# A hybrid RWKV-7 and pooling layer: the diagonal blocks of a chunk inverse picked and placed by DMA, and a decay polynomial in squared factors

## Chip, cores and metric

The kernel runs on one core of one Trainium2 chip. The metric is device time in microseconds (us) of one launch. Times of instructions are from one profiled execution; times of the kernel are medians of several runs.

## The reference, cut to what matters

One decoder layer over 1024 tokens of width 1024, in float32. The part that the change touches is the RWKV-7 time mixing of 8 heads of 64 channels:

```python
w_log = -jax.nn.softplus(-(w0 + jnp.tanh(wd) @ wl_up)) - 0.5
decay = jnp.exp(-jnp.exp(w_log))
...
def step(S, inp):
    r_t, w_t, k_t, v_t, a_t, b_t = inp
    Sa = jnp.einsum('bhvk,bhk->bhv', S, a_t)
    S = S * w_t[:, :, None, :] + Sa[..., None] * b_t[:, :, None, :] + v_t[..., None] * k_t[:, :, None, :]
    y = jnp.einsum('bhvk,bhk->bhv', S, r_t)
    return S, y
...
m = jnp.mean(y, axis=-1, keepdims=True)
var = jnp.mean(jnp.square(y - m), axis=-1, keepdims=True)
y = (y - m) * lax.rsqrt(var + GN_EPS) * lnx_g + lnx_b
```

Around it stand an input layer norm and projection, a pooling group, the output projection with its layer norm, a SwiGLU FFN with a gated embedding, and a last layer norm.

## The kernel before, in words

The program is written with tiles and pools; a scheduler orders the instructions of each engine ahead of time, and each engine, and the SP queue that issues nearly all DMAs, then works in that fixed order. `solve` is given high priority by the scheduler.

The recurrence runs in chunks of 64 tokens (`NC` = 8 chunks to a half sequence of 512). Work comes as eight tasks t = 0 to 7: four pairs of heads (`p`, 128 channels) for each half sequence (`s`). `fr(t)` projects or reloads r, k, v and calls `front`; `solve` is called for two tasks at a time, so there are four solves, called pair 0 to 3 here, and inside one the loop variable `q` (0 or 1) counts the two tasks. While a solve waits, the PE (TensorE) has projection matmuls `pz` to run and, towards the end of the phase, the output projection's `pm`.

- `front` (L352 to L423): the decay is a polynomial of degree six of a tanh `t1`. ACT makes the first factor (L369), five scalar_tensor_tensor steps on DVE follow (L371), ACT adds the constant (L375) and two scans on DVE make the running products (L377, L381).
- `gram` (L425 to L450): small matmuls `pg`, each evicted through a mask by DVE into `gB` and `gK` (L439).
- `inverse` (L452 to L532): in `gB` lies, for each of 16 chunk-and-head blocks of one task, a strictly triangular 64x64 matrix. Its four 16x16 diagonal blocks are inverted directly, 128 of them side by side, one to a partition. To get there DVE masks the matrix (`dg`, L462), folds it to 16 columns (`dc`, L464), a DMA writes `dc` to a DRAM scratch (L466), a second DMA reads it back regrouped into `ab` (L467), and DVE takes the diagonal blocks out of `gB` (L468). After the small steps on `ab` and `ef` (L478 to L502), one DMA for each task writes both the inverse and its transpose (L506), another reads them as `cc` (L508), and DVE spreads `cc` into the block-diagonal tiles `fx` and `ex` with a mask (L511). Then come 64x64 matmuls `pn` and `pzz` (L524 to L532).
- `chain` (L534 to L585): for each chunk in turn the matmuls `cw`, `cu`, `cs`, with a DVE copy or update between them.
- `post` (L587 to L606): group norm. ACT takes a reciprocal root of the variance (L596), DVE refines it by a Newton step (L597 to L599), scales `py` (L600), and applies gain, bias and gate (L601, L604).

Of the kernel before, what the change touches and what calls it, by code (L numbers as in the profile page):

```python
# [23 lines left out]
NC = 8  # L24
# [3 lines left out]
LN_EPS = 1e-5  # L28
GN_EPS = 1e-5 * 64

DECAY = [7.38403150e-01, -2.23932079e-01, 3.39554149e-02, -3.43247040e-03,
         2.60245296e-04, -1.58445669e-05, 7.95516283e-07]

MU, W0, A0, KK, KA, RK, LG, LB, PS, IG, IB, MG, MB = 0, 14, 18, 22, 26, 30, 34, 38, 42, 46, 54, 62, 70
NCOL = 78
# [7 lines left out]
def hybrid_layer(ctx, tc, x, pT, w_in, cols, rows, lora, gl, pool_w, w_out,  # L43
# [32 lines left out]
    for h in range(2):  # L76
        r = slice(64 * h, 64 * h + 64)
        G.affine_select(out=gmask[r, 0:64], in_=gmask[r, 0:64], pattern=[[1, 64]],
                        compare_op=ALU.is_gt, fill=0.0, base=0, channel_multiplier=-1)
        G.affine_select(out=gmask[r, 64:128], in_=gmask[r, 64:128], pattern=[[1, 64]],  # L80
                        compare_op=ALU.is_ge, fill=0.0, base=0, channel_multiplier=-1)
        G.affine_select(out=bmask[r, :], in_=bmask[r, :], pattern=[[-16, 4]],
                        compare_op=ALU.is_ge, fill=0.0, base=0, channel_multiplier=1)
        G.affine_select(out=bmask[r, :], in_=bmask[r, :], pattern=[[16, 4]],
                        compare_op=ALU.is_ge, fill=0.0, base=15, channel_multiplier=-1)
    e0 = cq.tile([128, 65 * NC + 1], F32, name="e0")
    V.memset(e0, 0.0)
    V.memset(e0[:, 0:65 * NC + 1:65], 1.0)
# [4 lines left out]
    V.memset(epsl, LN_EPS)  # L93
    epsg = cq.tile([128, 1], F32, name="epsg")
    V.memset(epsg, GN_EPS)
    qb = cq.tile([128, 2], F32, name="qb")
    V.memset(qb[:, 0:1], DECAY[5])
    V.memset(qb[:, 1:2], DECAY[0])

    col = cp.tile([128, NCOL], F32, name="col")  # L100
    nc.scalar.dma_start(col, cols)
# [8 lines left out]
    V.tensor_scalar(hka, col[:, KA:KA + 4], 0.5, None, ALU.mult)  # L110
    oka = cq.tile([128, 4], F32, name="oka")
    V.tensor_scalar(oka, col[:, KA:KA + 4], -0.5, 1.0, ALU.mult, ALU.add)
    lor = cq.tile([128, 512], F32, name="lor")
    glw = cq.tile([128, 512], F32, name="glw")

# [58 lines left out]
    with pa:  # L174
# [20 lines left out]
        def kb(name):  # L195
            return s1.tile([128, NC, 64], F32, name=name, tag="kb", bufs=3)
# [155 lines left out]
        def front(pair, q, p, s, r, k, v):  # L352
# [22 lines left out]
            S.activation(wx3[:, :, 1:65], v3(pc), AF.Identity, bias=qb[:, 1:2])  # L375
# [49 lines left out]
        def gram(pr):  # L425
# [14 lines left out]
            for q, d in enumerate(pr["t"]):  # L440

                bk = d["bk"]
                for g in range(2):
# [5 lines left out]
                                mm(pk[R, o:o + 64], bk[R, 4 * g + i, 64 * x:64 * x + 64], ident[R, 64 * h:64 * h + 64], True, True)  # L449
                    S.copy(kt2[:, q, 4 * g:4 * g + 4, :].rearrange("p c t -> p (c t)"), pk)  # L450

        def inverse(pr):  # L452

            gB = pr["gB"]
            abf = s1.tile([128, 272], F32, name="ab", tag="ab", bufs=1)
            ab = abf[:, 0:256].rearrange("b (s t) -> b s t", t=16)
            QR = HR
            for q in range(2):
                A4 = gB[:, q, :, 0:64].rearrange("p c (q t) -> p c q t", q=4)
                dg = kb("dg")  # L460
                dg4 = dg.rearrange("p c (q t) -> p c q t", q=4)
                V.tensor_tensor(dg4, A4, bmask[:, None, :, None].to_broadcast([128, NC, 4, 16]), ALU.mult)  # L462
                dc = s1.tile([128, NC, 16], F32, name="dc", tag="dc", bufs=2)
                V.tensor_reduce(dc, dg.rearrange("p c (q t) -> p c t q", q=4), AX.X, ALU.add)  # L464
                d1 = dp.tile([NC, 128, 16], F32, name="d1", tag="d1", bufs=4)
# [12 lines left out]
            for t in range(1, 4):  # L478
                tv = tm[:, 0:4 * t * t].rearrange("b (q i s) -> b q i s", q=4, s=t)
                V.tensor_tensor(tv, e4[:, :, 0:t, 0:t],  # L480
                                a4[:, :, None, 0:t, t].to_broadcast([128, 4, t, t]), ALU.mult)
                V.tensor_reduce(e4[:, :, 0:t, t:t + 1], tv, AX.X, ALU.add)

            def off(lo, n):

                mi, hi = lo + n, lo + 2 * n
                tv = tm[:, 0:n * n * n].rearrange("b (i t s) -> b i t s", t=n, s=n)
                w = e[:, mi:hi, lo:mi]
                V.tensor_tensor(tv, e[:, lo:mi, None, lo:mi].to_broadcast([128, n, n, n]),
                                ab[:, lo:mi, mi:hi].rearrange("b s t -> b t s")[:, None]  # L490
                                .to_broadcast([128, n, n, n]), ALU.mult)
# [12 lines left out]
            for q in range(2):  # L504
                d2 = dp.tile([2 * NC, 128, 16], F32, name="d2", tag="d2", bufs=4)
                nc.sync.dma_start(d2.rearrange("(x c) (a i) t -> (c a) x (i t)", x=2, i=16), ef[QR[q]])  # L506
                cc = s1.tile([128, 2 * NC, 16], F32, name="cc", tag="cc", bufs=2)
                nc.sync.dma_start(cc, d2.rearrange("g p t -> p g t"))  # L508
                E_, F_ = [s1.tile([128, NC, 64], F32, name=n, tag=n, bufs=2) for n in ("ex", "fx")]
                for i, t in ((1, F_), (0, E_)):  # L510
                    V.tensor_tensor(t.rearrange("p g (q t) -> p g q t", q=4),  # L511
                                    cc[:, NC * i:NC * i + NC, None, :].to_broadcast([128, NC, 4, 16]),
                                    bmask[:, None, :, None].to_broadcast([128, NC, 4, 16]), ALU.mult)
                EF.append((E_, F_))

            def diag(l, rr, nm):
                ps = psb(nm)
                for c in range(NC):
                    for R in HR:
                        mm(ps[R, 64 * c:64 * c + 64], l[R, c, :], rr[R, c, :], True, True)  # L520
                return v3(ps)


            for q, (E_, F_) in enumerate(EF):  # L524
                S.copy(F_, diag(gB[:, q, :, 0:64], F_, "pn"))
            rr = [E_ for E_, _ in EF]
            for i in range(3):
                for q, (E_, n1) in enumerate(EF):
                    pz = diag(n1, rr[q], "pzz")
                    if i != 1:  # L530
                        rr[q] = kb("rr") if i == 0 else gB[:, q, :, 0:64]
                    V.tensor_tensor(rr[q], pz, E_, ALU.add)  # L532
# [54 lines left out]
        def post(d, py):  # L587
# [13 lines left out]
            V.scalar_tensor_tensor(ys, ys, col[:, LG + p:LG + p + 1], d["bv"], ALU.mult, ALU.add)  # L601
# [572 lines left out]
```

## Time and profile before

| | before |
|---|---|
| median of 3 runs | 1360.7 us (1359.55 to 1363.9) |
| the profiled execution | 1362.55 us |
| its span | 1360.8 us |
| busy: PE, DVE, ACT, POOL | 96%, 75%, 39%, 1% |
| mean granted TensorE clock | 0.985 |
| DMA | 177.72 MB, 119405 packets, 34944 of them under 512 B |

Busy time of PE is modelled from matmuls that overlap, so a PE that is busy all the time need not be at its peak rate. The projections, the time mixing and the pooling end with the last `pm` at 594 us; the FFN follows, and its matmuls run back to back. The solves lie between 123 and 564 us.

### The profile page before, as it was taken

Reading aid. Unit: us, or ns where it says so; the run is one execution under the profiler, and the core shown is the slowest. Engines: PE = TensorE matmul, PEld = TensorE weight load, DVE = VectorE, ACT = ScalarE, POOL = GpSimd, SP = SyncE. Lnnn points to the kernel's source line nnn. Section 1 sums busy time; section 2 is a strip of 40 time slices with the busy share of each in tenths; the row PEclk is TensorE's granted clock in tenths of the full one; section 3 lists DMA queues with packets and bytes.
Section 4 is the critical chain, followed back from the end, with each engine's and each line's share of the span. In section 5 each row is a group of like instructions: output and inputs, shape, how many; then the busy total and the mean of one; then the engine's idle time right before and its main releaser. Section 6 shows DMA issues by size and latency. Waiting matters only on the chain.

```text
span 1360.8 us, 22957 instructions
## 1 busy us (share of the span) xinstructions
PE 1310.2 (96%) x9028; PEld 1033.7 (76%) x9028; DVE 1025.9 (75%) x1807; ACT 528.6 (39%) x889; POOL 12.7 (1%) x48
## 2 busy tenths in 40 slices
PE   7999999998997999989999999999999999999997
PEld 5787777776765667767888888888888888887886
DVE  6947566579698873557799999777667777988768
ACT  6723432244334521156634332333333334553530
POOL 0000000000000000000000000000000000000000
PEclk9999989999998999989999999999999999999999
DMA  8621130122124251475423346322232336997813
GB/s 275 221 102 51 54 75 10 59 78 61 35 57 119 83 150 55 133 235 185 148 94 123 101 139 210 131 101 102 79 107 101 102 123 218 322 310 251 268 33 124
DMA packets 119405, 177.72 MB, mean 131 GB/s; under 512 B 34944, under 2 KB 44160, under 8 KB 119296
## 3 DMA queue, kind: packets, MB, share of 16 engines
q1 hardware_dynamic: 119152, 176.20, 39.6%
q8 instruction: 71, 1.16, 0.3%
q14 instruction: 38, 0.31, 0.1%
q10 hardware_dynamic: 144, 0.04, 0.0%
HBM read 126.13 MB, written 50.07 MB: 129 GB/s over the span
## 4 chain that ended last, share of the span: by engine, by line
PE 72%; DVE 13%; DMA 10%; ACT 2%; issue 2%; SPq 0%; DVEq 0%; ACTq 0%
PE p L49 31%; PE pz L49 10%; PE py L49 6%; PE pgt L49 6%; PE px L49 4%; PE pm L49 3%; DMA wdr<-ff_down 2%; PE pg L49 2%; DMA o<-h_d 1%; PE cw L49 1%; PE pzz L49 1%; DMA ar<-a_d 1%; PE pe L49 1%; PE cs L49 1%; DMA m_d<-o 1%
## 5 line engine op out<-in xcount | busy, mean ns | idle before, releaser
L49 PE MATMUL p<-tb,p 128*128 128x512 f32 x1056 | 250.1, 392 | 0.0
L49 PEld LDWEIGHTS p<-tb,p 128*128 128x128 f32 x1056 | 198.5, 188 | 44.4
L49 PE MATMUL p<-h,p 128*128 128x512 f32 x792 | 191.1, 394 | 0.0
L49 PE MATMUL pz<-hT,wh 128*128 128x512 f32 x576 | 189.1, 403 | 0.0
L49 PEld LDWEIGHTS p<-h,p 128*128 128x128 f32 x792 | 149.2, 188 | 34.8
L792 ACT CAST p<-a 128x512 fp32r<-128x512 f32 x132 | 81.3, 622 | 183.6 <-PE p L49 145.4
L49 PEld LDWEIGHTS pz<-hT,wh 128*128 128x128 f32 x576 | 107.1, 188 | 31.8 <-issue 4.7
L49 PE MATMUL pz<-hT,wl 128*128 128x512 f32 x288 | 116.6, 405 | 0.0
L793 DVE TENSOR_TENSOR p<-a,p 128x512 fp32r<-128x512 f32 x132 | 89.3, 686 | 15.3 <-ACT p L792 14.9
L49 PE MATMUL pm<-wo,mh 128*128 128x512 f32 x224 | 77.3, 413 | 2.4 <-DVE o L751 1.4
L949 DVE TENSOR_TENSOR u<-p,u 128x512 f32<-128x512 f32 x66 | 45.3, 686 | 31.3 <-PE p L49 31.2
L49 PEld LDWEIGHTS pz<-hT,wl 128*128 128x128 f32 x288 | 54.0, 188 | 15.4 <-issue 3.8
L49 PE MATMUL px<-da 128*128 128x512 f32 x276 | 64.2, 389 | 0.0
L49 PEld LDWEIGHTS px<-da 128*128 128x128 f32 x276 | 51.8, 188 | 10.8
L49 PE MATMUL pgt<-wg,h 128*128 128x512 f32 x192 | 51.1, 412 | 2.7 <-ACT wg L792 2.6
L49 PEld LDWEIGHTS pm<-wo,mh 128*128 128x128 f32 x224 | 41.4, 188 | 14.6 <-DVE o L751 1.8
L235 DVE TENSOR_TENSOR wl<-wr,wh 128x512 fp32r<-128x512 f32 x36 | 24.7, 688 | 32.9 <-ACT wh L233 32.1
L49 PE MATMUL py<-da 128*128 128x512 f32 x204 | 47.6, 389 | 0.0
L49 PEld LDWEIGHTS pgt<-wg,h 128*128 128x128 f32 x192 | 37.4, 197 | 12.1 <-ACT wg L792 3.0
L49 PE MATMUL pm<-wo,ml 128*128 128x512 f32 x112 | 46.0, 413 | 0.0
L49 PEld LDWEIGHTS py<-da 128*128 128x128 f32 x204 | 38.3, 188 | 8.0
L970 DVE TENSOR_TENSOR gs<-p,u 128x512 f32<-128x512 f32 x44 | 30.3, 690 | 18.2 <-PE p L49 17.6
(321 smaller groups left out, 2342.4 us busy)
## 6 DMA issues: line engine op xcount, KB each, us to landing
ar<-a_d SPq DMA_DIRECT2D x77, 256.0 KB, 4.0
wdr<-ff_down SPq DMA_DIRECT2D x55, 256.0 KB, 3.9
a<-ff_gate SPq DMA_DIRECT2D x44, 256.0 KB, 2.8
a<-ff_up SPq DMA_DIRECT2D x44, 256.0 KB, 2.8
a_d<-s SPq DMA_DIRECT2D x44, 256.0 KB, 2.3
b<-ff_down SPq DMA_DIRECT2D x22, 512.0 KB, 5.5
wr<-w_in SPq DMA_DIRECT2D x36, 256.0 KB, 2.9
a_d<-gs SPq DMA_DIRECT2D x33, 256.0 KB, 2.2
```

The costliest lines, as they stand in the source:

```text
L49: PE.matmul(o, lhsT=l, rhs=r, start=a, stop=z)
L235: V.tensor_tensor(wl, wr, wh.bitcast(F32), ALU.subtract)
L792: S.copy(h, r)
L793: V.tensor_tensor(l, r, h.bitcast(F32), ALU.subtract)
L949: V.tensor_tensor(t, ps, u, ALU.add)
L970: V.tensor_tensor(d, ps, u, ALU.add)
```

## The change

Three edits, in `inverse`, `front` and `post`.

- In `inverse` the four DVE steps that pick and place the diagonal blocks go. Two DMAs for each task (one for each half of the partitions) write the 64x64 matrices from `gB` to a DRAM scratch with a row length of 64 words and 64 words of padding to a matrix, so that a view with a pitch of 1040 words meets just the diagonal blocks; one DMA reads them from there into `ab`. On the way back four DMAs for a pair write the blocks into four DRAM images `d2`, whose other words were set to zero once, ahead of the loop, and eight DMAs read whole 64-column rows into `ex` and `fx`. Off-diagonal cleaning of `gB` is one multiply by a mask `omask` for each task; it has to wait until the DMAs that read `gB` have ended.
- In `front` the decay polynomial is a product of squared terms: four ACT steps and two DVE steps in place of one and five.
- In `post` the Newton step takes the square from ACT: two DVE steps in place of three.

```diff
+        d2 = [[dp.tile([2 * NC * HS], F32, name=f"d2{q}{x}", bufs=1) for x in range(2)] for q in range(2)]
+        zt = s1.tile([128, 2 * NC * HS // 128], F32, name="zt", tag="k2", bufs=KA_BUFS)
+        G.memset(zt, 0.0)
+        for q in range(2):
+            for x in range(2):
+                nc.scalar.dma_start(d2[q][x].rearrange("(p r) -> p r", p=128), zt)
...
+        def rows_of(d, h):
+            return d.rearrange("(c h r) -> c h r", c=NC, h=2)[:, h, 0:64 * 64].rearrange("c (p t) -> p c t", t=64)
+        def blocks_of(d):
+            return d.rearrange("(g r) -> g r", g=64)[:, 0:1024].rearrange("g (s t) -> g s t", t=64)[:, :, 0:16]
...
-                V.tensor_tensor(dg4, A4, bmask[:, None, :, None].to_broadcast([128, NC, 4, 16]), ALU.mult)
-                V.tensor_reduce(dc, dg.rearrange("p c (q t) -> p c t q", q=4), AX.X, ALU.add)
-                nc.sync.dma_start(d1.rearrange("c p t -> p c t"), dc)
-                nc.sync.dma_start(abf[QR[q], 0:256], d1.rearrange("c (a s) t -> (c a) (s t)", a=8))
-                V.tensor_tensor(gB[:, q, :, 0:64], gB[:, q, :, 0:64], dg, ALU.subtract)
+                for h, R in enumerate(HR):
+                    nc.sync.dma_start(rows_of(d1, h), gB[R, q, :, 0:64])
+                nc.sync.dma_start(abf[QR[q], 0:256].rearrange("g (s t) -> g s t", t=16), blocks_of(d1))
...
-                nc.sync.dma_start(d2.rearrange("(x c) (a i) t -> (c a) x (i t)", x=2, i=16), ef[QR[q]])
-                nc.sync.dma_start(cc, d2.rearrange("g p t -> p g t"))
-                for i, t in ((1, F_), (0, E_)):
-                    V.tensor_tensor(t.rearrange("p g (q t) -> p g q t", q=4),
-                                    cc[:, NC * i:NC * i + NC, None, :].to_broadcast([128, NC, 4, 16]),
-                                    bmask[:, None, :, None].to_broadcast([128, NC, 4, 16]), ALU.mult)
+            for i in (1, 0):
+                for q in range(2):
+                    nc.sync.dma_start(blocks_of(d2[q][i]), ef[QR[q], i, :].rearrange("g (i t) -> g i t", t=16))
+                for q in range(2):
+                    for h, R in enumerate(HR):
+                        nc.sync.dma_start(EF[q][i][R], rows_of(d2[q][i], h))
+            for q in range(2):
+                V.tensor_tensor(gB[:, q, :, 0:64], gB[:, q, :, 0:64],
+                                omask[:, None, :].to_broadcast([128, NC, 64]), ALU.mult)
...
-            S.activation(pc, t1, AF.Identity, scale=DECAY[6], bias=qb[:, 0:1])
-            for n in (0.0, DECAY[4], DECAY[3], DECAY[2], DECAY[1]):
-                V.scalar_tensor_tensor(pc, pc, n, t1, ALU.add, ALU.mult)
+            S.activation(pc, t1, AF.Square, bias=qb[:, 0:1])
+            S.activation(pd, t1, AF.Square, bias=qb[:, 1:2])
+            S.activation(pd, pd, AF.Identity, bias=qb[:, 3:4])
+            S.activation(t1, t1, AF.Square, bias=qb[:, 2:3])
+            V.scalar_tensor_tensor(pc, pc, QE[0], pd, ALU.add, ALU.mult)
+            V.scalar_tensor_tensor(pc, t1, QE[2], pc, ALU.add, ALU.mult)
...
-            V.scalar_tensor_tensor(ys, pvv, GN_EPS, y0, ALU.add, ALU.mult)
-            V.scalar_tensor_tensor(ys, ys, -0.5, y0, ALU.mult, ALU.mult)
-            V.scalar_tensor_tensor(y0, ys, 1.5, y0, ALU.add, ALU.mult)
+            S.activation(ys, y0, AF.Square)
+            V.scalar_tensor_tensor(ys, pvv, GN_EPS, ys, ALU.add, ALU.mult)
+            V.scalar_tensor_tensor(y0, ys, 3.0, y0, ALU.subtract, ALU.mult)
```

Since the scheduler orders everything anew, rows also move. On the SP queue of pair 0, where the inverse goes out and comes back (`d_...` and `d2` are the DRAM scratch, `wr` a weight load for `pz`), there stood before:

```order
L616 DMA rkv_d<-k_1421 128x512
L506 DMA d_2130<-ef 64x2x256
L506 DMA d_2138<-ef 64x2x256
L231 DMA wr<-w_in 128x512
L508 DMA cc<-d_2130 128x16x16
L508 DMA cc<-d_2138 128x16x16
L616 DMA rkv_d<-v_1493 128x512
```

and now there stands (744 and 745 are the inverse and the transpose of the first task, 746 and 747 those of the second):

```order
L639 DMA rkv_d<-k_1439 128x512
L531 DMA d_744<-ef 64x16x16
L531 DMA d_745<-ef 64x16x16
L531 DMA d_747<-ef 64x16x16
L531 DMA d_746<-ef 64x16x16
L534 DMA ex<-d_744 64x8x64
L534 DMA fx<-d_745 64x8x64 x2
L534 DMA fx<-d_747 64x8x64 x2
L534 DMA ex<-d_744 64x8x64
L534 DMA ex<-d_746 64x8x64 x2
L639 DMA rkv_d<-v_1511 128x512
```

Twelve issues stand together where there were four, and the weight load that stood among them has moved behind. The other three pairs have the same twelve in a row.

On DVE, at the end of the gram of pair 0's second task (`gB`, `gK` are evictions of gram blocks, `tm` is the first small step on `ab`), there stood before:

```order
L439 TENSOR_TENSOR gB<-pg_1985,gmask 128x512
L439 TENSOR_TENSOR gK<-pg_1995,gmask 128x512
L462 TENSOR_TENSOR dg<-gB,bmask 128x512
L439 TENSOR_TENSOR gK<-pg_2005,gmask 128x512
L464 TENSOR_REDUCE dc<-dg 128x128
L468 TENSOR_TENSOR gB<-gB,dg 128x8x64
L480 TENSOR_TENSOR tm<-ef,ab 128x4
```

and now:

```order
L450 TENSOR_TENSOR gB<-pg_2005,gmask 128x512
L242 TENSOR_TENSOR wl<-wr,wh 128x512
L450 TENSOR_TENSOR gK<-pg_2015,gmask 128x512
L450 TENSOR_TENSOR gK<-pg_2025,gmask 128x512
L536 TENSOR_TENSOR gB<-gB,omask 128x8x64
L584 COPY ws<-cw 128x128
L502 TENSOR_TENSOR tm<-ef,ab 128x4
```

Between the last eviction of `gB` and the multiply by `omask` stand three steps here, four in the first tasks of pairs 0 and 2, and seven or more in the other five. On the PE the work is the same; behind the last `pgate` of pair 3 stood 131 `pm` matmuls, and now stand 91. On ACT two table loads come on, at the reciprocal root of `post`.

## Rows read from the trace of the kernel before

**Rows 1.** The page: busy time of the engines.
```profile
PE 1310.2 (96%) x9028; PEld 1033.7 (76%) x9028; DVE 1025.9 (75%) x1807; ACT 528.6 (39%) x889; POOL 12.7 (1%) x48
```
**Rows 2.** The chain of waits in order of time, the FFN: start, length, what.
```profile
714.69 415.89 PE p L49 x1800
```
**Rows 3.** A stretch: length, busy of PE, PEld, DVE, ACT, POOL, clock, DMA share, GB/s.
```profile
300.00:500.00 200.00, 182.25 (x2642) 132.09 (x2643) 172.07 (x353) 82.52 (x143) 5.55 (x18) 0.97 0.28 76
```
**Rows 4.** Groups by line, 100 to 600 us: busy, mean ns, idle before.
```profile
L371 DVE SCALAR_TENSOR_TENSOR pc<-pc,t 128x512 f32<-128x512 f32 x40 | 27.5, 688 | 10.7 <-ACT pc L369 10.3
...
L464 DVE TENSOR_REDUCE dc<-dg 128x128 f32<-128x512 f32 x8 | 8.2, 1027 | 0.0
...
L511 DVE TENSOR_TENSOR fx<-cc,bmask 128x512 f32<-128x512 f32 x8 | 5.5, 686 | 4.4 <-DMA cc<-d 4.4
...
L462 DVE TENSOR_TENSOR dg<-gB,bmask 128x512 f32<-128x512 f32 x8 | 5.5, 684 | 0.0
```
**Rows 5.** The chain of waits in order of time, pair 2.
```profile
377.81 0.96 DVE dc L464
378.76 0.60 DVE gB L468
...
380.56 0.60 DVE ys L598
...
392.87 0.60 DVE dg L462
...
394.67 0.95 DVE dc L464
...
408.78 0.60 DVE pc L371
...
412.27 0.09 DVE pc L371
...
417.80 0.61 DVE fx L511
```
**Rows 6.** The chain of waits in order of time, pair 1.
```profile
304.91 0.60 DVE dg L462
...
306.03 1.03 DVE dc L464
...
322.46 3.65 DMA cc<-d
...
326.13 0.69 DVE fx L511
...
328.03 0.60 DVE ex L511
```
**Rows 7.** The chain of waits in order of time, pair 3.
```profile
468.12 0.95 DVE dc L464
469.07 0.60 DVE gB L468
...
482.75 0.95 DVE dc L464
```
**Rows 8.** Issues by the SP queue for these tiles: time of one, least/median/most ns.
```profile
L466 SPq DMA_DIRECT2D d<-dc x8: 371/374/383, 129.5 to 483.7; - x8
...
L506 SPq DMA_DIRECT2D d<-ef x8: 607/618/651, 188.6 to 499.9; - x8
```
**Rows 9.** DMAs: KB each, median us from issue to landing.
```profile
d<-ef SPq DMA_DIRECT2D x8, 128.0 KB, 2.5
cc<-d SPq DMA_DIRECT2D x8, 128.0 KB, 4.0
...
d<-dc SPq DMA_DIRECT2D x8, 64.0 KB, 2.3
ab<-d SPq DMA_DIRECT2D x8, 64.0 KB, 2.1
```
**Rows 10.** The SP queue in order of time, pair 0: start, length of both issues.
```profile
191.10 1.85 SPq L508 DMA_DIRECT2D cc<-d  x2
```

More of the change, by code (lines that the diff above doesn't have):

```diff
@@ L29 @@
 GN_EPS = 1e-5 * 64
-DECAY = [7.38403150e-01, -2.23932079e-01, 3.39554149e-02, -3.43247040e-03,
-         2.60245296e-04, -1.58445669e-05, 7.95516283e-07]
+QB = [2.6446236909266547, -4.777402204072105, -7.825890616949517]
+QE = [148.19110777287312, 64.07475031771858, 7.586255131509925]
+QS = 7.95516283e-07
 MU, W0, A0, KK, KA, RK, LG, LB, PS, IG, IB, MG, MB = 0, 14, 18, 22, 26, 30, 34, 38, 42, 46, 54, 62, 70
@@ L85, in hybrid_layer @@
                         compare_op=ALU.is_ge, fill=0.0, base=15, channel_multiplier=-1)
+    omask = cq.tile([128, 64], F32, name="omask")
+    V.tensor_scalar(omask.rearrange("p (q t) -> p q t", q=4), bmask[:, :, None].to_broadcast([128, 4, 16]),
+                    -1.0, 1.0, ALU.mult, ALU.add)
     e0 = cq.tile([128, 65 * NC + 1], F32, name="e0")
@@ L95, in hybrid_layer @@
     V.memset(epsg, GN_EPS)
-    qb = cq.tile([128, 2], F32, name="qb")
-    V.memset(qb[:, 0:1], DECAY[5])
-    V.memset(qb[:, 1:2], DECAY[0])
+    qb = cq.tile([128, 4], F32, name="qb")
+    for i, c in enumerate(QB + [QE[1]]):
+        V.memset(qb[:, i:i + 1], c)
     col = cp.tile([128, NCOL], F32, name="col")
@@ L112, in hybrid_layer @@
     V.tensor_scalar(oka, col[:, KA:KA + 4], -0.5, 1.0, ALU.mult, ALU.add)
+    hlg = cq.tile([128, 4], F32, name="hlg")
+    V.tensor_scalar(hlg, col[:, LG:LG + 4], -0.5, None, ALU.mult)
     lor = cq.tile([128, 512], F32, name="lor")
@@ L368, in front @@
             pc = k2("pc")
-            S.activation(pc, t1, AF.Identity, scale=DECAY[6], bias=qb[:, 0:1])
-            for n in (0.0, DECAY[4], DECAY[3], DECAY[2], DECAY[1]):
-                V.scalar_tensor_tensor(pc, pc, n, t1, ALU.add, ALU.mult)
+            pd = k2("pd")
+            S.activation(pc, t1, AF.Square, bias=qb[:, 0:1])
[4 more added lines that the diff above has]
+            V.scalar_tensor_tensor(pc, t1, QE[2], pc, ALU.add, ALU.mult)
             wx = k2("wx", w=65 * NC + 1)
@@ L374, in front @@
             wx3 = wx[:, 0:65 * NC].rearrange("p (c t) -> p c t", t=65)
-            S.activation(wx3[:, :, 1:65], v3(pc), AF.Identity, bias=qb[:, 1:2])
+            S.activation(wx3[:, :, 1:65], v3(pc), AF.Copy, scale=QS)
             Ep = s2.tile([128, NC, 65], F32, name="Ep", tag="ep", bufs=1)
@@ L450, in gram @@
                     S.copy(kt2[:, q, 4 * g:4 * g + 4, :].rearrange("p c t -> p (c t)"), pk)
+        HS = 64 * 64 + 64
+        def rows_of(d, h):
[8 more added lines that the diff above has]
+                nc.scalar.dma_start(d2[q][x].rearrange("(p r) -> p r", p=128), zt)
         def inverse(pr):
@@ L458, in inverse @@
             for q in range(2):
-                A4 = gB[:, q, :, 0:64].rearrange("p c (q t) -> p c q t", q=4)
-                dg = kb("dg")
-                dg4 = dg.rearrange("p c (q t) -> p c q t", q=4)
-                V.tensor_tensor(dg4, A4, bmask[:, None, :, None].to_broadcast([128, NC, 4, 16]), ALU.mult)
-                dc = s1.tile([128, NC, 16], F32, name="dc", tag="dc", bufs=2)
-                V.tensor_reduce(dc, dg.rearrange("p c (q t) -> p c t q", q=4), AX.X, ALU.add)
-                d1 = dp.tile([NC, 128, 16], F32, name="d1", tag="d1", bufs=4)
-                nc.sync.dma_start(d1.rearrange("c p t -> p c t"), dc)
-                nc.sync.dma_start(abf[QR[q], 0:256], d1.rearrange("c (a s) t -> (c a) (s t)", a=8))
-                V.tensor_tensor(gB[:, q, :, 0:64], gB[:, q, :, 0:64], dg, ALU.subtract)
+                d1 = dp.tile([2 * NC * HS], F32, name="d1", tag="d1", bufs=4)
+                for h, R in enumerate(HR):
+                    nc.sync.dma_start(rows_of(d1, h), gB[R, q, :, 0:64])
+                nc.sync.dma_start(abf[QR[q], 0:256].rearrange("g (s t) -> g s t", t=16), blocks_of(d1))
             eff = s1.tile([128, 528], F32, name="ef", tag="ef", bufs=1)
@@ L504, in inverse @@
             for q in range(2):
-                d2 = dp.tile([2 * NC, 128, 16], F32, name="d2", tag="d2", bufs=4)
-                nc.sync.dma_start(d2.rearrange("(x c) (a i) t -> (c a) x (i t)", x=2, i=16), ef[QR[q]])
-                cc = s1.tile([128, 2 * NC, 16], F32, name="cc", tag="cc", bufs=2)
-                nc.sync.dma_start(cc, d2.rearrange("g p t -> p g t"))
                 E_, F_ = [s1.tile([128, NC, 64], F32, name=n, tag=n, bufs=2) for n in ("ex", "fx")]
-                for i, t in ((1, F_), (0, E_)):
-                    V.tensor_tensor(t.rearrange("p g (q t) -> p g q t", q=4),
-                                    cc[:, NC * i:NC * i + NC, None, :].to_broadcast([128, NC, 4, 16]),
-                                    bmask[:, None, :, None].to_broadcast([128, NC, 4, 16]), ALU.mult)
                 EF.append((E_, F_))
+            for i in (1, 0):
[7 more added lines that the diff above has]
+                                omask[:, None, :].to_broadcast([128, NC, 64]), ALU.mult)
             def diag(l, rr, nm):
@@ L596, in post @@
             S.activation(y0, pvv, AF.Abs_reciprocal_sqrt, bias=epsg)
-            V.scalar_tensor_tensor(ys, pvv, GN_EPS, y0, ALU.add, ALU.mult)
-            V.scalar_tensor_tensor(ys, ys, -0.5, y0, ALU.mult, ALU.mult)
-            V.scalar_tensor_tensor(y0, ys, 1.5, y0, ALU.add, ALU.mult)
+            S.activation(ys, y0, AF.Square)
+            V.scalar_tensor_tensor(ys, pvv, GN_EPS, ys, ALU.add, ALU.mult)
+            V.scalar_tensor_tensor(y0, ys, 3.0, y0, ALU.subtract, ALU.mult)
             V.tensor_tensor(ys, py, y0, ALU.mult)
-            V.scalar_tensor_tensor(ys, ys, col[:, LG + p:LG + p + 1], d["bv"], ALU.mult, ALU.add)
+            V.scalar_tensor_tensor(ys, ys, hlg[:, p:p + 1], d["bv"], ALU.mult, ALU.add)
             pg = chp.tile([128, 512], F32, name="pgate", tag="ch")
```

## The prediction

> **What bounds the kernel now.** I read the busy times first, then the chain of waits in order of time, then the groups by line and the DMAs. PE is busy 96% of the span, DVE 75% and ACT 39% [rows 1], which looks like a kernel that only PE can slow down. The FFN bears this out: 1800 matmuls in 415.89 us are 0.231 us each, one behind the other [rows 2], and no edit here touches it. But those 96% are modelled from overlapping matmuls. Between 300 and 500 us, where pairs 1 to 3 are solved, PE is called busy for 182 of 200 us with many small matmuls among them, while DVE is busy for 172 [rows 3], 86% in place of its mean of 75%. The chain of waits says who holds whom: in pair 2 it runs on DVE from step to step, with a step every 0.60 us although one lasts 0.69 us by itself [rows 5, 4]. A step every 0.60 us means that the next one was already waiting for DVE. So the solves from pair 1 on are paced by DVE's backlog and by the two DMA relays of the inverse, and PE has too little to run beside them. Before 300 us projections cover most of this, and DVE's steps there are largely off the path.
>
> **Change, part by part: DVE.** In each of eight tasks the inverse drops `dg`, the fold `dc`, the subtraction and two expansions, and gains the multiply by `omask`: at the pace of a backlog 4 x 0.60 + 0.95 - 0.60 = 2.75 us [rows 5], so 22.0 us in all. The decay drops three of five steps, 8 x 3 x 0.60 = 14.4 us, and the norm one of three, 4.8 us. That is 41.2 us of DVE time, and only what lies on the chain counts:
>
> - Pair 2: `dc` 0.96, the subtraction 0.60, one step of the norm 0.60, `dg` 0.60, `dc` 0.95, together 3.71; the five pieces of `pc` from 408.78 to 412.27 are 0.60 + 0.55 + 0.60 + 0.66 + 0.09 = 2.50, of which three fifths, 1.50, go; `fx` 0.61. Sum 5.82 us [rows 5].
> - Pair 1: `dg` 0.60, `dc` 1.03, and the four expansions from 326.13 to the one at 328.03, 0.69 + 0.25 + 0.69 + 0.60. Sum 3.86 us [rows 6].
> - Pair 3: 0.95 + 0.60 + 0.95 = 2.50 us [rows 7].
> - Pair 0: one expansion, 0.69 us [rows 4], since PE waits for the first `fx` there too; the rest is covered by projections.
>
> Together 12.9 us come off. The `omask` multiply puts 0.60 us back at three of these places (first task of pair 2, both of pair 3): 1.8 us. It also waits until the DMAs that read `gB` have landed; with seven or more steps of 0.60 us ahead of it that costs nothing, and with three or four at most 0.37 + 2.3 - 1.8 = 0.9 us [rows 8, 9], in pair 0 mostly in front of a step that waits for `ab` anyway. I take nothing.
>
> **ACT.** Three more steps a task in the decay and one in the norm, some 0.7 us each, and two more table loads lie on an engine that is busy 39% [rows 1]. The decay's latency doesn't grow, because four ACT steps and two DVE steps stand where one and five stood. I cost this at nothing; what hides it is ACT's idle time, and without that cover it would be about 3 us a task.
>
> **First relay, `gB` to `ab`.** Two writes where there was one, so one more issue of 0.37 us [rows 8] ahead of the read. The trace has no such read, 1024 pieces of 64 bytes. It lies between `ab`'s 2.1 us now (64 long pieces) and `cc`'s 4.0 us (2048 pieces of 64 bytes) [rows 9]. I take the middle, 3.05 us, since the count is half of `cc`'s. That adds 0.37 + 0.95 = 1.3 us; in pairs 1 to 3, where PE cannot cover it, 3.9 us. The ends are 0.37 and 2.3 us a pair.
>
> **Second relay, `ef` to `ex` and `fx`.** Now: two writes, 2.5 us to landing, then the read of `cc`, whose second issue starts 0.93 us behind the first (1.85 us for two), 4.0 us, then one expansion of 0.69 us [rows 9, 10]: the second task's `fx` is there 8.1 us after `ef`. With the change, twelve issues stand in one row, and the last half of the second `fx` is the ninth: at 0.62 us an issue [rows 8] it starts after 5.0 us, and lands, as a 64 KB transfer of the 2.3 us kind or a `cc` of 4.0 us [rows 9], 7.3 to 9.0 us after `ef`. I take no change; the ends are -0.8 and, with issues of 0.93 us throughout (7.4 + 4.0 = 11.4 us), +3.3 us a pair. The zero images are written once, during projections, by ACT's queue, and cost nothing there.
>
> **PE's order.** Behind the last `pgate` stand 91 `pm` matmuls in place of 131. Forty at 0.231 us [rows 2] are 9.2 us that now lie inside the solves. They are free where PE waited for a solve anyway, and a mere exchange where it didn't: ends 9.2 and 0 us. I take half, 4.6 us.
>
> **Sum.** -12.9 + 1.8 + 3.9 - 4.6 = -11.8 us against the profiled execution's own 1362.55 us (its span is 1360.8 us): 1350.8 us. That execution is 1.85 us above the median of the runs shown, 1360.7 us; I predict **1350 us**.
>
> **Rivals.**
>
> *Slower: the relays are the new wait.* The place is the SP queue behind `ef`, which issues in order: the twelve transfers stand behind each other, and `fx` and the weight loads behind them. If an issue with a thousand short pieces takes 0.93 us [rows 10] and its landing 4.0 us, the second relay gains 3.3 us and the first 0.37 + 1.9 = 2.3 us a pair, four pairs 22 us, and nothing is left over for the 40 matmuls: 1362.55 - 12.9 + 1.8 + 22 = 1373 us. It decides from 2.8 us a pair on, where 11.1 us of relief are eaten up. For it speaks that all of the new transfers consist of pieces of 64 or 256 bytes, and that pair 2 has little PE work ready between `cw` and `pn`; against it, that 1024 pieces of 64 bytes land in 2.3 us and 64 long ones of the same 64 KB in 2.1 us [rows 9]. The Trainium skill (DMA: Bandwidth & Descriptors, Specifications) asks for transfers of at least 512 bytes, since below that an engine reads, modifies and writes; by that rule the DRAM writes of `ef`, now cut into 64 bytes, would be the late ones. The two rows just named show no such penalty. Chance 0.21.
>
> *No change: PE sets the pace after all.* Then DVE's relief only lets it wait longer for the same matmuls, and the time stays near 1361 us. For it: 96% busy [rows 1]; against it: the chain goes through DVE for long stretches of pairs 2 and 3 [rows 5, 7]. Chance 0.13.
>
> *Faster still: DVE's backlog is a rate.* Then what leaves DVE between 300 and 500 us counts in full, whether or not the chain names it: about two and a half solves (2.5 x 5.5), four fronts (4 x 1.8) and four norms (4 x 0.6), 23 us, less the 3.9 us of the first relay. The time would be 1362.55 - 19 = 1343 us, and 1334 us with all 40 matmuls for free. For it: 86% busy there [rows 3]; against it: the relays, which no lighter DVE shortens. Chance 0.18.
>
> **How the numbers follow.** The forecast has 0.48. A measurement of this kernel can tell some 0.3%, 4.1 us, from no change. Faster by more: 0.48 + 0.18 = 0.66; within: 0.13; slower by more: 0.21. The range goes from the best case, 1334 us, up through no change and into the slower rival, to 1368 us, half way to its full price; that leaves out about 2 in 10.
>
> **What would show it.** Right: DVE busy 41 us less over the span; SP issues of the twelve near 0.6 us; from `ef`'s last copy to the second task's first `pn` about 8 us; less idle time of PE between 300 and 564 us. Wrong: issues near 0.9 us or landings of 4 us and more, `omask` with DVE idle ahead of it, and PE waiting longer for `fx`; then the slower rival holds. If PE's idle time is the same and DVE's has grown by 41 us, it is no change.

## The result and the profile after

The change makes the kernel slower: 1370.58 us median (1364.77 to 1375.15, 6 runs) against 1360.12 us (1358.62 to 1363.9, 6 runs), a ratio of 1.0067, 95% interval 1.0042 to 1.0091. A second set, in the experiments below, gave 1.0074 (1.0056 to 1.0092). The prediction was 1350 us with a range up to 1368. The profiled execution of after took 1371.18 us, its span is 1369.5 us.

What was taken from DVE is gone. The page's busy times, as [rows 1]:

```profile
PE 1318.5 (96%) x9028; PEld 1031.8 (75%) x9028; DVE 984.2 (72%) x1747; ACT 548.8 (40%) x923; POOL 13.6 (1%) x49
```

DVE has 41.7 us less work (41.2 predicted), ACT 20 us more. In the stretch of [rows 3] DVE falls from 172 to 143 us. So the edit did its first step in full, and the time went the other way. Where? The same view (length, busy of PE, PEld, DVE, ACT, POOL, clock, DMA share, GB/s), first two stretches of before:

```profile
400.00:450.00 50.00, 42.99 (x680) 30.03 (x678) 42.07 (x95) 27.11 (x47) 1.85 (x6) 0.93 0.38 106
600.00:655.00 55.00, 50.72 (x222) 40.07 (x221) 36.02 (x65) 39.47 (x59) 0.00 (x0) 0.88 0.52 172
```

and of after:

```profile
300.00:500.00 200.00, 183.49 (x2545) 128.59 (x2543) 142.70 (x292) 91.41 (x157) 4.85 (x17) 0.95 0.34 90
...
400.00:450.00 50.00, 36.24 (x518) 24.67 (x520) 36.41 (x73) 24.44 (x38) 1.74 (x5) 0.80 0.33 87
600.00:655.00 55.00, 47.33 (x196) 36.68 (x195) 34.50 (x63) 39.02 (x54) 0.00 (x0) 0.84 0.58 196
```

PE runs 518 matmuls instead of 680 between 400 and 450 us, the granted clock falls from 0.93 to 0.80, and DVE is *less* busy too: both engines wait. That is the inverse of pair 2. Taken from its last masked `gB` eviction to its last `pzz`, in before and then in after:

```profile
391.60:427.60 36.00, 29.75 (x500) 21.41 (x498) 32.85 (x68) 17.98 (x27) 1.84 (x6) 0.91 0.36 88
```

```profile
394.30:445.80 51.50, 37.48 (x495) 24.19 (x497) 37.25 (x72) 25.72 (x40) 1.74 (x5) 0.80 0.38 100
```

Almost the same number of matmuls (500 and 495) in 15.5 us more.

The solves are a row of stages, one behind the other, so a ledger can be made of the trace: the time between the first or last starts of the instructions that bound a stage, summed over the four pairs.

| stage (sum of four pairs, us) | before | after | |
|---|---|---|---|
| last `gB` eviction to first step on `ab` (first relay) | 36.8 | 35.0 | -1.8 |
| DVE steps on `ab` and `ef`, to `ef`'s last copy | 34.2 | 39.7 | +5.5 |
| `ef`'s copy to the first `pn` (second relay) | 31.8 | 31.4 | -0.4 |
| first `pn` to last `pzz` (the products) | 44.0 | 69.3 | **+25.3** |
| last `pzz` to the next pair's last `gB` eviction (pair 3: to the last `pgate`) | 244.9 | 231.5 | -13.4 |
| last `pgate` to the FFN's first `pgt` | 43.8 | 37.2 | -6.6 |

With +0.3 us ahead of the first stage and -0.1 us behind the last this makes up the 8.7 us between the spans, but for rounding. The two stages that hold the relays did not grow. The products behind the second one take 25 us more. The DVE steps take 5.5 us more, 4.4 of them in pair 2 (from 9.1 to 13.5 us), where steps of the norm and of a front stand between the small ones. The two later stages are 20 us shorter.

The row of the second relay ends with the first task's first `pn`. The second task's first `pn` comes 37.2 us behind `ef`'s copy in before and 47.2 in after, summed over the pairs. Pair 3 shows how. Matmuls in order of time (start, length, what, idle time before and what ended it), before:

```profile
507.80 2.35 PE L49 MATMUL pn<-fx,gB 64*64 64x64 f32 x64 [0.90 <-DVE fx L511]
509.96 2.03 PE L49 MATMUL pzz<-ex,fx 64*64 64x64 f32 x62
512.37 0.33 PE L49 MATMUL pzz<-ex,fx 64*64 64x64 f32 x2 [0.39 <-issue]
514.17 5.49 PE L49 MATMUL pzz<-rr,fx 64*64 64x64 f32 x128 [1.47 <-DVE rr L532]
```

and after:

```profile
517.35 0.29 PE L51 MATMUL pn<-fx,gB 64*64 64x64 f32 x2 [0.49 <-DMA fx<-d]
...
519.37 1.14 PE L51 MATMUL pn<-fx,gB 64*64 64x64 f32 x30
520.45 0.51 PE L51 MATMUL pm<-wo,ml 128*128 128x512 f32 x1
520.79 0.63 PE L51 MATMUL pm<-wo,mh 128*128 128x512 f32 x2
521.35 0.33 PE L51 MATMUL pn<-fx,gB 64*64 64x64 f32 x2
...
523.08 1.14 PE L51 MATMUL pn<-fx,gB 64*64 64x64 f32 x30
...
525.04 1.14 PE L51 MATMUL pzz<-ex,fx 64*64 64x64 f32 x30
526.11 0.50 PE L51 MATMUL pm<-wo,mh 128*128 128x512 f32 x1
```

Products that ran as one block are cut up, with `pm` between the pieces. Matmuls of other parts that stand there are called fillers here. From the first `pn` to the last `pzz` of a pair the trace has 22 `pz`, 18 `pz`, 3 `pm` and 27 `pm` in pairs 0 to 3; before it had one `pz` in all. And PE did not wait for the data. The waits of PE between 180 and 540 us (what, for what, us in all, times, longest) have one row with a transfer of the relays, the last of these:

```profile
PE pm L51 <- ACT mh L760: 7.5, 1, 7.5
PE pbo L51 <- DVE rb L422: 2.9, 3, 2.0
PE pzz L51 <- DVE rr L555: 2.3, 2, 1.6
...
PE pn L51 <- DMA fx<-d: 0.5, 1, 0.5
```

Half a microsecond, once, and none for `ex`. PE took what its order had next. The order is fixed ahead of time, and each engine follows it. The Trainium skill (PSUM — Partial Sum Buffer, Engine vs sequencer instructions) says that matmuls start in program order, and that the queues of ScalarE, VectorE and GpSimd are strictly first in, first out. The rows agree: the last `fx` issue of this pair starts at 516.1 us and such a transfer lands after 3.4, so it was there by about 519.5; the second task's `pn` starts at 521.35 and its main block at 523.08.

The other pairs are alike. The last image, the second half of the second task's `ex`, lands 10.9 to 11.9 us behind `ef`'s copy, which is 3.1 to 4.3 us behind the first `pn`. The last `pzz` starts 12.5 to 16.3 us after that landing, though a whole block of products from first `pn` to last `pzz` takes 7.9 to 9.5 us where it is left in one piece (e5 below).

The relays' own rows (KB each, median us from issue to landing), as [rows 9]:

```profile
d<-gB SPq DMA_DIRECT2D x16, 128.0 KB, 2.6
ex<-d SPq DMA_DIRECT2D x16, 128.0 KB, 3.6
fx<-d SPq DMA_DIRECT2D x16, 128.0 KB, 3.4
d<-ef SPq DMA_DIRECT2D x16, 64.0 KB, 2.6
ab<-d SPq DMA_DIRECT2D x8, 64.0 KB, 2.7
```

Issues of `fx` and `ex` take 0.61 and 0.63 us, as taken.

### The profile page after: what moved, and what is told of

The parts are those of the page before. It is cut to its first block, busy times and chain, and to the rows that moved or that the text cites. A ratio compares the mean times of both kernels' runs of the same rounds, so it can differ in the third digit from the quotient of the medians.

```text
span 1369.5 us, 22998 instructions
## 1 busy us (share of the span) xinstructions
PE 1318.5 (96%) x9028; PEld 1031.8 (75%) x9028; DVE 984.2 (72%) x1747; ACT 548.8 (40%) x923; POOL 13.6 (1%) x49
## 4 chain that ended last, share of the span: by engine, by line
PE 81%; DVE 8%; DMA 5%; ACT 4%; issue 2%; SPq 0%; DVEq 0%; ACTq 0%
PE p L51 31%; PE pz L51 12%; PE pgt L51 7%; PE py L51 6%; PE px L51 6%; PE pm L51 4%; PE pg L51 2%; PE pzz L51 2%; PE cw L51 1%; PE cs L51 1%; PE pk L51 1%; PE pn L51 1%; PE cu L51 1%; PE pe L51 1%; PE pt L171 1%
## 5 line engine op out<-in xcount | busy, mean ns | idle before, releaser
L51 PE MATMUL pm<-wo,mh 128*128 128x512 f32 x224 | 81.3, 428 | 8.1 <-ACT mh L760 7.5
L51 PEld LDWEIGHTS px<-da 128*128 128x128 f32 x276 | 51.8, 188 | 10.8
L51 PEld LDWEIGHTS pm<-wo,mh 128*128 128x128 f32 x224 | 41.7, 191 | 20.4 <-issue 9.9
L993 DVE TENSOR_TENSOR gs<-p,u 128x512 f32<-128x512 f32 x44 | 30.3, 689 | 18.5 <-PE p L51 18.0
```

Source lines behind the costliest of these rows:

```text
L51: PE.matmul(o, lhsT=l, rhs=r, start=a, stop=z)
L993: V.tensor_tensor(d, ps, u, ALU.add)
```

## Experiments

The theories, as numbered in the expectations: **1**, DVE's relief pulls fronts, projections and pools forward, and pair 2's inverse is left without PE work; **2**, the first relay is the new wait (in the expectations of e1 to e4: the relays are); **3**, the second relay costs the time, **3a** through the order laid out for it, **3b** because its data is late. The last column is the sum over four pairs from `ef`'s copy to the last `pzz`. Each ratio is to runs of before made beside that kernel, so kernels from different rows compare by their ratios:

| run | median us | ratio to before (95%) | ef to pzz |
|---|---|---|---|
| before | | 1 | 75.8 |
| after | 1370.58 | 1.0067 (1.0042 to 1.0091) | 100.5 |
| e1 inverse alone | 1373.33 | 1.0091 (1.0066 to 1.0116) | 100.4 |
| e2 decay and norm alone | 1355.97 | 0.9964 (0.9943 to 0.9985) | 69.2 |
| e3 decay alone | 1358.17 | 0.9978 (0.9963 to 0.9993) | 69.6 |
| e4 norm alone | 1360.34 | 0.999 (0.9975 to 1.0005) | 74.4 |
| e5 second relay undone | 1357.19 | 0.9967 (0.9954 to 0.998) | 64.1 |
| e6 first relay undone | 1374.71 | 1.01 (1.0068 to 1.0132) | 102.1 |
| e7 `ex` on ACT's queue | 1377.45 | 1.0119 (1.0083 to 1.0154) | 92.4 |
| e8 pool group 0 held | 1368.18 | 1.0041 (1.0022 to 1.006) | 101.3 |
| e9 `pn` waits for all | 1378.42 | 1.0127 (1.0109 to 1.0146) | 112.3 |
| e10 before, relay split | 1367.77 | 1.0046 (1.0029 to 1.0064) | 73.9 |
| e11 fillers held on PE | 1377.45 | 1.0113 (1.0094 to 1.0132) | 92.1 |
| e12 after again | 1372.17 | 1.0074 (1.0056 to 1.0092) | 99.0 |
| e13 eight DMAs | 1380.75 | 1.014 (1.0115 to 1.0164) | 109.4 |
| e14 reads of 2 KB, blocks not placed | 1355.29 | 0.9956 (0.9935 to 0.9977) | 71.9 |
| e15 order on three engines | 1364.82 | 1.003 (1.0016 to 1.0044) | 81.3 |
| e16 e5 with e15's order | 1356.73 | 0.9955 (0.9936 to 0.9975) | 67.1 |

### Which edit: e1 to e4

Parts of the change's diff, put on the kernel before: e1 takes all of `inverse`, `omask` and the zeroed images; e3 `QB`, `QE`, `QS` and the four squares in `front`; e4 the lines of `post` and `hlg`; e2 is e3 and e4.

> The inverse's edit alone (diagonal blocks by DMA, omask, zeroed images); decay and group norm as in the kernel before. Theory 1 (order: the time is set by which fillers lie beside pair 2's inverse): the relays themselves cost no more than the vector work that they replace, so this is between 1352 and 1364 us, and the stretch of pair 2 from its last gB to its last pzz, 36.0 us before and 51.5 after, is under 42 us wherever the time is under 1362 us. Theory 2 (relays: the twelve small DMAs of a pair's inverse are the new wait): the whole loss stays, 1368 us or more, and the stretch of every pair from ef's copy to the first pn is over 9 us.

> Decay and group norm as changed; the inverse as before. Theory 1 (order): relief of VectorE alone pulls fronts 5 to 7 forward too (pw of front 7 before 435 us, 440.2 before the change), so part of the loss or at least no gain shows: 1357 to 1372 us. Theory 2 (relays): without relays only the relief of some 19 us of VectorE work is left, so it is faster than before, 1352 us or less.

> The decay's edit alone (three scalar_tensor_tensor fewer and three activations more in each of eight fronts, some 14 us of VectorE). Theory 1 (order): 1355 to 1370 us, with pair 2's inverse (last gB to last pzz) longer than 40 us where the time is above 1363. Theory 2 (relays): 1351 to 1356 us, since nothing here makes a relay.

> The group norm's edit alone (one VectorE step of 0.6 us less and one activation more in each of eight posts, some 5 us of VectorE). Both theories: within 4 us of the kernel before, 1356 to 1364 us; theory 1 allows either sign, theory 2 only a gain.

The inverse alone loses 12.3 us, decay and norm alone win 5.1, so the loss is the inverse's. Theory 1 missed e1 (1352 to 1364 expected), and e2 lies between the two theories' ranges (1357 to 1372, and 1352 or less). Theory 1 holds e3, theory 2 missed it (1351 to 1356). Theory 2 named the right edit but `ef`'s copy to the first `pn` is 8.1 us or less in every pair of e1, and not over 9 as it said.

### Which relay: e5 and e6

e5 puts the old lines back behind `ef`, e6 those ahead of `ab`:

```diff
 e5, from after
-            for i in (1, 0):
-                for q in range(2):
-                    nc.sync.dma_start(blocks_of(d2[q][i]), ef[QR[q], i, :]...)
-                ...
+                nc.sync.dma_start(d2.rearrange(...), ef[QR[q]])
+                nc.sync.dma_start(cc, d2.rearrange("g p t -> p g t"))
+                ...
 e6, from after
-                for h, R in enumerate(HR):
-                    nc.sync.dma_start(rows_of(d1, h), gB[R, q, :, 0:64])
+                V.tensor_tensor(dg4, A4, bmask..., ALU.mult)
+                V.tensor_reduce(dc, ..., AX.X, ALU.add)
+                ...
```

> After with the second relay undone (cc through one image and the masked products on VectorE, as before); first relay, omask, decay and norm stay as changed. Theory 3 (the second relay lands its four images one after the other, and the products pn and pzz of each pair are spread over 16 to 19 us instead of 9 to 14): the stretch from the first pn to the last pzz goes back to 8 to 12 us in each pair, and the time to 1354 us or less. Theory 1 (only the lead of fronts 5 to 7 matters, whichever part of the relief gives it): 1358 to 1370 us. Theory 2 (the first relay's 3 us a pair are the loss): 1366 us or more, with gB's last write to tm's first over 10 us in each pair.

> After with the first relay undone (dg, dc and the subtraction on VectorE, d1 as before, no omask); the second relay, decay and norm stay as changed. Theory 3: the loss stays, 1368 us or more, with first pn to last pzz at 15 us or more in every pair. Theory 2: it goes, 1352 us or less. Theory 1: between, since VectorE has part of its work back, 1358 to 1366 us.

This decides between the relays. Without the second the kernel is faster than before (1357.2 us, 3 us over the 1354 that theory 3 gave); with the second and without the first it is the slowest so far. Beside e2, the same kernel without either relay, the first adds 1.2 us and the second 18.7 (by the ratios 0.4 and 18.5). The first is inside the intervals of both. In e5 the products of pair 1 are one block again (first and last start behind the three durations, then the form):

```profile
L51 PE MATMUL pn<-fx,gB x64: 218/218/267, 321.7 to 324.5; 64*64 64x64 f32 x64
...
L51 PE MATMUL pzz<-rr,fx x128: 218/218/267, 326.6 to 331.1; 64*64 64x64 f32 x128
```

From 321.7 to 331.1 us are 9.4 us; in after the same rows go from 327.0 to 342.9, 16 us.

### How the second relay costs: e7 to e12

```diff
 e7, from after: i = 0 is E, i = 1 is F
+            qe = (nc.scalar, nc.sync)
-                    nc.sync.dma_start(...)
+                    qe[i].dma_start(...)
 e8, from after, pool group 0 only
+                one = s1.tile([128, 1], F32, name="one", bufs=1)
+                V.tensor_scalar(one, tk[2]["kt"][:, 1, 7, 64:65], 0.0, 1.0, ALU.mult, ALU.add)
-                S.copy(wh, wr)
+                S.activation(wh, wr, AF.Copy, scale=one)
 e9, from after, behind the omask step
+            for q in range(2):
+                V.scalar_tensor_tensor(EF[q][1][:, 0, 0:1], EF[1][0][:, 0, 0:1], 0.0, EF[q][1][:, 0, 0:1], ALU.mult, ALU.add)
 e10, from before
+            for i in (1, 0):
+                for q, (d2, cc) in enumerate(dcs):
+                    nc.sync.dma_start(d2[NC * i:NC * i + NC].rearrange(...), ef[QR[q], i, :])
+                for q, (d2, cc) in enumerate(dcs):
+                    for R in HR:
+                        nc.sync.dma_start(cc[R, NC * i:NC * i + NC], d2[NC * i:NC * i + NC, R]...)
 e11, from after: the n-th pz or pm matmul, from a given n on
+            with tc.issue_after(held[pair]):
+                mm(*a)
```

> After with the E half of the second relay (d from ef, and ex from d) issued from ScalarE's queue beside the F half on SyncE's, so that the landings overlap; nothing else changes. Theory 3: first pn to last pzz shrinks to 9 to 13 us in pairs 1 to 3, and the time to 1361 us or less. Theories 1 and 2: unchanged within 3 us of after, 1367 to 1374 us, since neither VectorE's relief nor the first relay is touched.

> After with the 48 pz matmuls of pool group 0 held back until pair 2's kt is there (a scale of one made from kt in their weights' cast), so that TensorE has them in pair 2's inverse. Theory 1 (pair 2's inverse lacks TensorE work): the granted clock of 400 to 450 us, 0.80, goes to 0.9 or more, and the time to 1364 us or less. Theory 3: the pair's chain is as long as before and the products are as spread; within 3 us of after, 1367 to 1375 us.

> After with two steps of one element a partition that make F of both halves depend on the last landing of E, so that pn starts only when all four images are there, and the products of a pair follow each other on TensorE. Theory 3a (the images are there early enough, but TensorE's instruction order, laid out beforehand, has 18 to 27 filler matmuls between a pair's products): the first pn to the last pzz is 8 to 11 us in each pair instead of 16 to 19, the start of pn is some 3 us or more later, and the time is 3 to 10 us less than after, 1361 to 1368 us. Theory 3b (the twelve DMAs themselves are late, the products could not run earlier anyway): the last pzz is where it was and the time is within 3 us of after, 1368 to 1374 us.

> The kernel before, its second relay split into the same twelve DMAs (four writes, one per half and image; eight reads of 64 partitions, F's first), the masked products on VectorE as before. Theory 3b: the number and order of the DMAs is what costs, so the time is 8 us or more over the kernel before, 1368 us or more. Theory 3a: its order has 0 to 3 filler matmuls between a pair's products, so within 4 us of the kernel before, 1357 to 1365 us.

> After with nothing changed but TensorE's order: pz matmuls from the 528th (pair 0) and the 792nd on (pair 1) and pm matmuls from the 132nd on (pair 3) are queued behind the last pzz of that pair, with no wait for data; so of the fillers between the first pn and the last pzz, 22, 18 and 27 of them, none or one is left. Theory 3a: that stretch falls to 8 to 12 us in pairs 0, 1 and 3, and the time by 6 to 16 us, to 1355 to 1364 us. Theory 3b: TensorE then waits for fx or ex there, and the time stays within 3 us of after. Theory 1: the same work is moved to other places of TensorE's order, so unchanged within 3 us of after.

> The changed kernel again, beside the three others on the same chip: 1367 to 1374 us by every theory.

**e7** missed: the products shrink by 11 us in sum, but the kernel is slower than after. Fillers fall from 70 to 29, and now PE does wait for `fx`: 18.7 us in six places, 6.8 at most, where it was 0.5. The edit also holds ACT, which takes its own work and these issues in one order. In pair 0 a weight cast stands 5.6 us behind the two writes of `ef`, which wait for `ef`; in pair 1 the four reads of `ex` take 3.9 us of ACT's queue. So e7 does not part order from landing.

**e8** is the test of theory 1. The clock between 400 and 450 us rises to 0.90 as expected, and the time falls by 2 to 4 us, with intervals that meet after's, and not to 1364 us: the 48 matmuls are missing between 350 and 400 us instead, where PE's busy time falls from 49.67 to 39.83 us. Moving filler moves the wait. Theory 1 describes where the loss shows, not what makes it.

**e9** makes the products compact (39.8 us in four pairs), but `pn` starts 72.5 us in sum behind `ef`'s copy, not the 31.4 of after plus some 3 a pair. The landing alone does not explain that: in pair 1 the last image lands at 331.0 us, and the two added DVE steps, which stand behind the next front's in DVE's order, run at 336.7. Both theories missed it.

**e10** has the twelve DMAs and yet unchanged products (44.1 us). It is 5.9 us slower than before, 0.2 us under what 3b gave and 2.8 us over 3a's range. In its trace the growth stands in pair 2's DVE steps, 17.1 us from the first one to `ef`'s copy against 9.1, with steps of front 6 among them. That this is what costs is not shown: e5 and e14 have 15.0 us there and are faster than before.

**e11** missed most clearly. Its edit names matmuls only (and puts the first solve one front earlier in the program), but the orders of DVE, ACT and SP change with it. Nearly all of the 67 fillers are gone from between the products, and pairs 0 and 1 are no faster (17.7 and 16.0 us). In pair 1 PE now idles there; its waits from 332 to 350 us:

```profile
PE pzz L51 <- ACT fx L564: 2.7, 1, 2.7
PE pn L51 <- DMA fx<-d: 1.2, 2, 0.8
```

ACT's copy of `pn` stands behind the next front's activations in ACT's order, `rr` behind its DVE steps. So what was laid between the products is not matmuls alone, and to hold back one engine's part only lets that engine wait. In e7 and e11 the stretch from `ef` to `pzz` is 8 us shorter than in after and the kernel 5 to 7 us slower, so a shorter stretch is not by itself a shorter time.

### Order or landing: e13 to e16

```diff
 e13, from after: E and F in one image, xf[:, 0] and xf[:, 1]
-                        nc.sync.dma_start(EF[q][i][R], rows_of(d2[q][i], h))
+                    nc.sync.dma_start(xf[R].rearrange("p x c t -> p (x c) t"), d2b[q]...[:, h]...)
 e14, from after
-                        nc.sync.dma_start(EF[q][i][R], rows_of(d2[q][i], h))
+                        nc.sync.dma_start(EF[q][i][R].rearrange("p c t -> p (c t)"), d2[q][i]...[h, 0:64 * 512].rearrange("(p r) -> p r", p=64))
 e15, from e11: in front, from pq on (fronts 2 and 7) or from ss on (front 4)
+                    for ins in (held[after], ends["ACT"][after], ends["DVE"][after]):
+                        hs.enter_context(tc.issue_after(ins))
 e16: e15 with e5's second relay
```

> After with E's and F's images in one, read by one DMA per half and image pair: four writes and four reads (each of twice the bytes, the same 256-byte pieces) in place of four and eight. If the number of DMAs costs (issue on SyncE, 0.6 us each): 4 to 10 us less than after, 1361 to 1367 us. If landing time or the order laid out for it costs: no gain, 1368 us or more, since its order has as many fillers between the products (28, 16, 2 and 38 matmuls).

> After with the eight reads of the second relay taking one contiguous piece of 2 KB per partition, from the same images; what is read is not the placed blocks, so E and F hold other values. Twelve DMAs as before, 64 pieces instead of 512 per read. Its order has 2, 8, 0 and 5 filler matmuls between a pair's products. If pieces are what makes the relay dear (landing, and the order laid out for it): 1358 us or less, with first pn to last pzz at 12 us or less in each pair, and ex landing well under the 3.6 us of after. If the number of DMAs: 1366 us or more.

> After, all DMAs as they are, with the order alone changed on three engines: the fillers pz and pm as in the run before that held them, and the steps of fronts 2, 4 and 7 that stood between a pair's products queued behind that pair's last product step on TensorE, ScalarE and VectorE. Order theory (the images are there in time): ef's copy to the last pzz is 20 us or less in each pair, 80 in all, against 101 in after and 76 before the change, and the time is 1366 us or less. Landing theory (the images are late): PE then waits for DMA fx and ex, the sum stays over 92 us, and the time over 1368 us.

> The second relay undone (as in the run with the first relay alone, 1357 us) and the order of e15 on three engines: the steps of fronts 2, 4 and 7 queued behind the products of the pair before them. If a lighter order in pair 2 (tm to ef at 15.0 us there, 7.2 in e15) still pays where nothing stands between the products: 1349 to 1354 us. If fillers and steps are only moved from one stage to the next: 1355 to 1362 us.

**e15** changes no transfer's form and no arithmetic, only orders. The edit sets those of PE, ACT and DVE; SP's changes with them, and two of ACT's 25 table loads go. It takes `ef` to `pzz` from about 100 to 81.3 us and the ratio from 1.0074 to 1.003: 5 to 6 of the 10 us. Not all of that need be the products': the DVE steps ahead of `ef`'s copy fall from 39.7 to 32.5 us in sum, and the stage behind the last `pzz` grows by 19 us. Now PE does wait for the images, 0.5 us in all in after and here:

```profile
PE pn L51 <- DMA fx<-d: 11.4, 8, 8.2
```

8.2 us of it are one place, pair 2's first `pn`, where PE's order has no other matmul ahead of it; the rest is 0.2 to 0.9 us each. But the products still take 52.9 us against 44.0 in before, which speaks for a part of the late landing of the later images. Pair 1 in order of time:

```profile
328.38 0.33 PE L51 MATMUL pn<-fx,gB 64*64 64x64 f32 x2 [0.50 <-DMA fx<-d]
329.08 1.15 PE L51 MATMUL pn<-fx,gB 64*64 64x64 f32 x32 [0.38 <-DMA fx<-d]
...
331.88 1.18 PE L51 MATMUL pzz<-ex,fx 64*64 64x64 f32 x32
...
334.75 1.10 PE L51 MATMUL pzz<-ex,fx 64*64 64x64 f32 x30
```

The landings bound that part. In after the last image lands 45.0 us behind `ef`'s copy, summed over the pairs. Products that waited for it and then ran in one piece as in e5 (35.9 us) would make a stretch of 81 us. By this estimate, of the 36 us between after's 100.5 and e5's 64.1 at most 17 are landing and some 20 are order. e15's 81.3 fits it. It divides the stretch, not the time at the end.

**e14** keeps twelve DMAs and the bytes, but leaves out the placing: `ex` and `fx` hold other values, so it is a test of time only. It reads each image half in 64 pieces of 2 KB instead of 512 of 256 bytes. Its issues and landings:

```profile
L534 SPq DMA_DIRECT2D ex<-d x16: 540/596/618, 194.2 to 508.5; - x16
DMA to landing us min/median/max: 2.6/2.9/3.4
```

2.9 us, where `fx` and `ex` took 3.4 and 3.6. The Trainium skill (DMA: Bandwidth & Descriptors, Why small descriptors are slow (HBM only)) says that small pieces carry a fixed overhead each, 27% of the bus cycles at 256 bytes. The direction agrees: the differences, 0.5 of 3.4 and 0.7 of 3.6 us, are 15% and 19% of a landing, and how much of a landing is that bus no run here shows. The time falls to 1355.3 us, some 16 us for 0.5 to 0.7 us a landing. The order changed with the form of the reads: it has 2, 8, 0 and 5 fillers between a pair's products, and they take 45.0 us. **e13** is the counterpart: eight DMAs with the old pieces, 28, 16, 2 and 38 fillers, 73.5 us of products and the slowest run of all. Fewer DMAs do not help where each lands later, here after 5.8 us.

**e16**: where nothing stands between the products, e15's order brings nothing more (0.9955 against e5's 0.9967), although the DVE steps ahead of `ef`'s copy are shorter here too, 32.3 us against e5's 42.8. e2, e5 and e16 all beat both kernels, and by the intervals they are one time; e2, decay and norm alone, is the simplest of them.

## Why the prediction was wrong

- *DVE's relief*: right in amount, 41.7 us for 41.2. e2 turns its 19 us of it into 5.1 us of time, where the chain's 12.9 us had 2.1 for these two edits (0.60 and 1.50 in pair 2). The other 10.8 us are the inverse's and come only together with the relays; no run tests them alone.
- *`omask`*: DVE waited 3.5 us in all for the DMAs that read `gB`, in two places, 1.8 us at most. Taken at nothing with up to 0.9 us a place, it was under-priced, but small.
- *ACT*: costed at nothing, with the decay's latency unchanged. DVE did wait longer for it, 32.5 us in five places for `pd` where it had been 10.3 for `pc` [rows 4], but e3, the decay alone, is still faster than before (0.9978).
- *First relay*: issues of 0.62 us (0.37 taken) and a landing of the read of 2.7 us (3.05 taken). Together with the shorter way to it the stage is 1.8 us shorter in four pairs, and e5 against e2 prices the whole first relay, relief and waits, at 1.2 us, which is inside the intervals. The +3.9 us were no great error.
- ***Second relay*: the step that failed.** "I take no change" was worked out for the second task's `fx`, the ninth transfer of twelve. For the data that held: the last `fx` lands 8.8 to 9.7 us behind `ef`'s copy, inside the bound of 11.4, and the issues were as taken. But the forecast's own sign, the second task's first `pn` about 8 us behind the copy, failed: it came after 11.6 to 12.2 us, with the data there 2 to 3 us before. And the stage does not end there. `pzz` needs `ex`, whose last three issues come behind, and the four images now arrive one after the other. In the order laid out for these transfers 70 `pz` and `pm` matmuls and steps of the next front stand between the products of a pair. The price, +25.3 us on the products, had no term in the sum and no place in the bounds of +3.3 us a pair: e5 and e6 put what the second relay costs at the end at 13 to 19 us.
- *PE's order*: -4.6 us was taken for 40 `pm` matmuls that moved up. The tail did become 6.6 us shorter. But 27 `pm`, 6.2 us at 0.231 us each, now stand between pair 3's products, where before PE stood idle for 1.9 us (the 0.39 and 1.47 above), and pair 2 had less PE work than before (518 matmuls for 680).
- *The rival "the relays are the new wait"* gave 1373 us and the right queue and tile. Its mechanism did not hold: issues were 0.61 to 0.63 us and not 0.93, and PE waited for `fx` 0.5 us. That its number comes near the measured one is luck.

What stays open: e15 gives back 5 to 6 us by orders and e14 some 16 by pieces, landing and order at once. How much of the time is landing alone no run separates, since any change to the transfers changed the order as well; the 17 and 20 us above are an estimate for the stretch. What makes e10's twelve DMAs 5.9 us dearer with the products unchanged was not found.

## What to carry to other kernels

Price a relay up to the last transfer that its consumer stage needs, not to the first use. When one read is replaced by several that land in turn, look at the new order of every in-order engine between the first and the last use: what stands there will be run even if the data is early, and here it delayed the chain on three engines at once. Filler matmuls that "move up" are a gain only where the profile shows the engine idle; check which later stage they leave empty.

## What was not expected of the hardware

The same 128 KB landed in 2.9 us in 2 KB pieces and in 3.4 to 3.6 us in 256-byte pieces; 64 KB written in 64-byte pieces landed in 2.6 us, and 128 KB in longer ones, before, in 2.5, so any penalty for short writes is small here. Twice the bytes in one DMA of 256-byte pieces (e13's `xf`) took 5.8 us. And a DMA queue moved to ACT was not free for ACT: in e7 a cast stood 5.6 us behind two writes that had to wait for their data, and four issues took 3.9 us of ACT's queue.
